# Input slices of 2, 2, 4, 4 and 4 blocks, more partial sums, wide products and new distances in a hybrid RWKV-7 and attention block

## The chip, the cores and the metric

The kernel runs on one core of a Trainium2 chip. The metric is the time of one execution in microseconds (us) on the device; the times shown are medians of several executions. The core's engines are named as the profile names them: PE multiplies matrices (PEld is its loading of weights), DVE is the vector engine, ACT the scalar engine, POOL the general one, SP issues most of the DMA transfers.

## What is computed

One sequence of 256 tokens with 2048 channels passes through one block, in float32:

```python
mod = silu(c) @ w_ada + b_ada                 # (2048) x (2048, 12288)
sh1, sc1, gt1, sh2, sc2, gt2 = split(mod, 6)
h = rms_norm(x) * (1 + sc1) + sh1
p = h @ w_in + b_in                           # (256, 2048) x (2048, 8736)
y_rwkv = rwkv7_branch(p[:, :3360], ...)       # 16 heads of 64: r, k, v; low ranks for decay, rate, gate
y_attn = sliding_window_attention(p[:, 3360:4640])   # 16 query heads, 2 key/value heads, window 128
g_rwkv, g_attn = split(sigmoid(p[:, 4640:]), 2)
merged = g_rwkv * (y_rwkv @ w_branch_rwkv) + g_attn * (y_attn @ w_branch_attn)
x = x + gt1 * (merged @ w_out)
h = rms_norm(x) * (1 + sc2) + sh2
x = x + gt2 * (square(relu(h @ w_up)) @ w_down)      # 2048 -> 8192 -> 2048
out = rms_norm(x)
```

The RWKV recurrence over 256 steps is done in chunks of 64 tokens; within a chunk a triangular system is inverted, first in blocks of 16.

## The kernel before

**Products.** Every weight matrix is read once, in tiles of 0.52 MB (four blocks of 128 rows by 256 columns, or two by 512). `split` (L269) loads such a tile (raw, L290), ACT rounds it into whi (L278), and DVE subtracts to get the remainder wlo (L279); there are seven buffers for raw, which the tiles of w_ada share, and four each for whi and wlo. The activations are kept as two parts too (hA and hB, side by side in one tile h). `feed` (L282) then issues for each 128x128 piece three matmuls of 256 columns (L301): whi by the high part, whi by the low part, wlo by the high part. This is the narrow form, 24 matmuls a tile, and gates, keys and branches use it through `cols_product`. The up projection of the MLP uses a wide form (`up_pair`, L1173): whi by both parts at once, 512 columns, and wlo by the high part, 16 matmuls a tile; the two halves of the result are added afterwards, by a copy on ACT (L1191) and an add on DVE (L1192) for each 128 columns.

**Input slices.** h depends on sc1 and sh1, which come from w_ada. So the 16 blocks of 128 channels are taken in slices, `SL`. For the first slice PE multiplies the ada tiles (L204); for the later ones DVE accumulates them (`ada_dve`, L223) while PE works on the slice before, and PE adds up the columns at the end (L190). Each slice contributes to 16 column pairs of w_in (256 columns each). Six are kept in PSUM throughout (three tiles each with two pairs), and ten are summed in SBUF (`sums`): a product over the slice's blocks only, copied by ACT in the first slice (L974) and added by DVE later (L976).

**Streams beside the products.** The modulation of the next slice, the attention and the RWKV branch are generators. `pulse` is called once a tile and advances each by a rate (`RATE_ADA`, `RATE_ATT`, `RATE_RW`, `RATE_BG`), so their instructions stand among those of the products; on each engine the order is then fixed. After the fourth sum of the last slice the heads of the RWKV branch and the attention begin.

**After the slices** come gates 4 to 6, `keyed(2)` and `keyed(3)` (k, r and v of the later head groups, written to a DRAM buffer that the second half of the RWKV branch reads), gate 7, eight pairs of an attention gate and an attention branch product, eight RWKV branch products, w_out, and the MLP.

**The inverse.** `inverse16` (L615) runs twice, once in each half of the RWKV branch. The blocks of 16 are written to a DRAM buffer scr, read back as lg, worked on by 31 small operations on POOL (L626, L628, L630; 15 to 64 elements per partition, then 256), written to DRAM and read back as in; then PE uses them (L651).

Of the kernel before, what the change touches and what calls it, by code (L numbers as in the profile page):

```python
# [85 lines left out]
def hybrid_block(ctx: ExitStack, tc, x, c, w_ada, b_ada, norm1_gain, w_in, b_in, rwkv_mix, rwkv_w0,  # L86
# [181 lines left out]

    def split(nk, width, load):  # L269

        step = max(1, 1024 // width)
# [10 lines left out]
    def feed(w, k0, nk, cols, blocks, xh, xl, begin, end, tw=T):  # L282
# [11 lines left out]
        for a, n, hi, lo in split(nk, width, load):  # L294
            for wt, xs in ((hi, (xh, xl)), (lo, (xh,))):
                for kk in range(n):
                    k = k0 + a + kk
                    o = 0
                    for ps, j, m in blocks:
                        for xx in xs:  # L300
                            TE.matmul(ps[0:m, j * tw:(j + 1) * tw], lhsT=wt[:, kk, o:o + m], rhs=xx(k),  # L301
                                      start=(k == begin and xx is xh and wt is hi and j == 0),
                                      stop=(k == end and wt is lo), skip_group_check=True)
                        o += m
# [303 lines left out]
    def zero_inverses():  # L608
        z = arena[0][:, 2 * W3:2 * W3 + BP // 2]
        G.memset(z, 0.0)  # L610
        for n in range(2):
# [678 lines left out]
```

## Time and profile before

| | us |
|---|---|
| median of 3 executions | 1543.69 |
| lowest and highest | 1542.36, 1549.06 |
| the profiled execution's own time | 1539.98 |
| its span in the trace | 1538.2 |
| PE busy | 1477.7 |
| DVE busy | 1119.0 |
| ACT busy | 724.0 |
| POOL busy | 40.1 |

The span is what the trace covers of the execution; a busy time is the union of an engine's instructions, and what is missing to the span is idle. The mean granted clock of PE was 0.988. The windows further below cut the span at the first w_in product (40.68 us), at the starts of the next slices (91.46, 143.13, 193.5), and behind the RWKV branch products (711); from 711 on come w_out and the MLP.

### The profile page before, as it was taken

Reading aid. Unit: us, or ns where it says so; the run is one execution under the profiler, and the core shown is the slowest. Engines: PE = TensorE matmul, PEld = TensorE weight load, DVE = VectorE, ACT = ScalarE, POOL = GpSimd, SP = SyncE. Lnnn points to the kernel's source line nnn. Section 1 sums busy time; section 2 is a strip of 40 time slices with the busy share of each in tenths; the row PEclk is TensorE's granted clock in tenths of the full one; section 3 lists DMA queues with packets and bytes.
Section 4 is the critical chain, followed back from the end, with each engine's and each line's share of the span. In section 5 each row is a group of like instructions: output and inputs, shape, how many; then the busy total and the mean of one; then the engine's idle time right before and its main releaser. Section 6 shows DMA issues by size and latency. Waiting matters only on the chain.

```text
span 1538.2 us, 28406 instructions
## 1 busy us (share of the span) xinstructions
PE 1477.7 (96%) x11194; PEld 1313.8 (85%) x11194; DVE 1119.0 (73%) x1842; ACT 724.0 (47%) x1136; POOL 40.1 (3%) x97
## 2 busy tenths in 40 slices
PE   5899999999999989999899999999999999999997
PEld 2898998998998989899789888888888888888885
DVE  1989979977688948768679765766676675655676
ACT  3354477656364424444457544434344343444443
POOL 2000000030000030000000000000000000000000
PEclk9899999999999999999999999999999999999999
DMA  9999977779898768879775777677776776666652
GB/s 345 338 342 306 350 237 229 239 200 316 251 291 282 239 182 296 269 255 310 246 236 165 241 230 236 213 233 231 228 231 213 236 231 204 190 191 193 203 183 79
DMA packets 297093, 372.68 MB, mean 242 GB/s; under 512 B 40912, under 2 KB 198384, under 8 KB 296320
## 3 DMA queue, kind: packets, MB, share of 16 engines
q1 hardware_dynamic: 296448, 370.72, 75.8%
q8 instruction: 88, 1.44, 0.4%
q0 software_dynamic: 512, 0.15, 0.1%
q14 instruction: 45, 0.37, 0.1%
HBM read 357.96 MB, written 12.86 MB: 241 GB/s over the span
## 4 chain that ended last, share of the span: by engine, by line
PE 84%; DVE 6%; DMA 4%; issue 2%; ACT 2%; POOL 1%; SPq 0%; DVEq 0%; POOLq 0%; ACTq 0%
PE mm L1173 21%; PE mm L301 19%; PE mm L323 14%; PE ax L323 14%; PE ax L301 7%; DMA ada<-in_w_ada_dram 2%; DVE acc L223 2%; DVE wlo L279 1%; PE ax L690 1%; PE ax L484 1%; PE ax L190 1%; PE ax L573 1%; DMA raw<-in_w_in_dram 1%; DMA tt<-in_x_dram 0%; POOL p L628 0%
## 5 line engine op out<-in xcount | busy, mean ns | idle before, releaser
L278 ACT CAST whi<-raw 128x1024 fp32r<-128x1024 f32 x458 | 478.9, 1049 | 591.1 <-PE ax L323 220.2
L279 DVE TENSOR_TENSOR wlo<-raw,whi 128x1024 fp32r<-128x1024 f32 x458 | 556.6, 1219 | 210.3 <-ACT whi L278 206.2
L223 DVE SCALAR_TENSOR_TENSOR acc<-ada,cact,acc 128x512 f32<-128x512 f32 x330 | 247.1, 749 | 90.7 <-DMA ada<-in_w_ada_dram 86.3
L1173 PE MATMUL mm<-h,whi 128*128 128x512 f32 x928 | 235.0, 395 | 0.0
L301 PE MATMUL mm<-h,whi 128*128 128x256 f32 (+1 forms) x1440 | 196.9, 285 | 3.4 <-ACT whi L278 3.4
L1173 PEld LDWEIGHTS mm<-h,whi 128*128 128x128 f32 x928 | 166.2, 188 | 31.5
L301 PEld LDWEIGHTS mm<-h,whi 128*128 128x128 f32 (+1 forms) x1440 | 178.0, 189 | 9.7 <-issue 3.5
L323 PE MATMUL mm<-whi,u 128*128 128x512 f32 x512 | 137.3, 390 | 0.0
L323 PE MATMUL ax<-whi,u 128*128 128x512 f32 x512 | 136.9, 389 | 0.0
L1173 PEld LDWEIGHTS mm<-h,wlo 128*128 128x128 f32 x928 | 123.2, 188 | 10.5
L1173 PE MATMUL mm<-h,wlo 128*128 128x256 f32 x928 | 124.8, 277 | 0.0
L301 PE MATMUL ax<-h,whi 128*128 128x256 f32 x768 | 105.7, 286 | 8.8 <-DVE p L976 5.1
L323 PEld LDWEIGHTS ax<-whi,u 128*128 128x128 f32 x512 | 96.1, 188 | 20.0
L323 PEld LDWEIGHTS mm<-whi,u 128*128 128x128 f32 x512 | 95.4, 188 | 19.4
L301 PEld LDWEIGHTS ax<-h,whi 128*128 128x128 f32 x768 | 96.9, 192 | 11.1 <-ACT whi L278 6.6
L301 PE MATMUL mm<-h,wlo 128*128 128x256 f32 (+1 forms) x720 | 103.7, 281 | 0.0
L301 PEld LDWEIGHTS mm<-h,wlo 128*128 128x128 f32 (+1 forms) x720 | 92.4, 189 | 0.4 <-DVE wlo L279 0.2
L323 PE MATMUL ax<-wlo,u 128*128 128x512 f32 x256 | 78.8, 389 | 0.0
L323 PE MATMUL mm<-wlo,u 128*128 128x512 f32 x256 | 78.8, 389 | 0.0
L301 PE MATMUL ax<-h,wlo 128*128 128x256 f32 x384 | 57.9, 283 | 0.1
L323 PEld LDWEIGHTS ax<-wlo,u 128*128 128x128 f32 x256 | 48.0, 188 | 10.0
L323 PEld LDWEIGHTS mm<-wlo,u 128*128 128x128 f32 x256 | 48.1, 188 | 10.0
(350 smaller groups left out, 1668.0 us busy)
## 6 DMA issues: line engine op xcount, KB each, us to landing
ada<-in_w_ada_dram SPq DMA_DIRECT2D x192, 512.0 KB, 5.6
raw<-in_w_up_dram SPq DMA_DIRECT2D x128, 512.0 KB, 4.1
raw<-in_w_down_dram SPq DMA_DIRECT2D x128, 512.0 KB, 4.2
raw<-in_w_in_dram SPq DMA_DIRECT2D x72, 512.0 KB, 5.7
raw<-in_w_in_dram SPq DMA_DIRECT2D x128, 256.0 KB, 5.7
raw<-in_w_out_dram SPq DMA_DIRECT2D x32, 512.0 KB, 5.0
raw<-in_w_branch_attn_dram SPq DMA_DIRECT2D x16, 512.0 KB, 6.0
raw<-in_w_branch_rwkv_dram SPq DMA_DIRECT2D x16, 512.0 KB, 5.3
```

The source lines that it names most:

```text
L190: TE.matmul(ps[:, j:j + 1], lhsT=acc[:, j * P:(j + 1) * P], rhs=ones[:, 0:1], start=True, stop=True)
L223: V.scalar_tensor_tensor(o, in0=t[:, a, :], scalar=ck, in1=o, op0=ALU.mult, op1=ALU.add)
L278: S.copy(hi[:], raw[:])
L279: V.tensor_tensor(lo[:], raw[:], hi[:].bitcast(F32), op=ALU.subtract)
L301: TE.matmul(ps[0:m, j * tw:(j + 1) * tw], lhsT=wt[:, kk, o:o + m], rhs=xx(k), start=(k == begin and xx is xh and wt is hi and j == 0), sto ...
L323: TE.matmul(pss[tb][:], lhsT=uu(k)[:, sl], rhs=wt[:, kk, :], start=(first and k == 0), stop=(final and k == kblocks - 1))
L484: TE.matmul(out[hs, :], lhsT=src[hs, chunk(c)], rhs=ident[hs, hs], start=True, stop=True)
L573: TE.matmul(pT[hs, o:o + P], lhsT=src[hs, chunk(c)], rhs=ar[hs, i, c].rearrange("p a b -> p (a b)"), start=True, stop=True)
L690: TE.matmul(ps[hs, j, i, part, :], lhsT=lhs(j, i, hs), rhs=rhs(j, i, hs), start=(first and j == 0 and i == 0), stop=True, skip_group_check ...
L1173: TE.matmul(pss[j][:, 0:w_], lhsT=wt[:, kk, j * P:(j + 1) * P], rhs=xx(a + kk), start=(a + kk == 0 and wt is hi), stop=(a + kk == KC - 1 a ...
```

## The change

The input is taken in five slices, the first two of two blocks. Ada tiles of a slice of two hold four blocks of rows by 256 columns instead of two by 512. Three pairs join the sums, those of `keyed(2)`; after the last slice they go to the DRAM buffer, and the later product goes. For slices of four, `feed` takes one pair at a time, and with `apart=True` it finishes one PSUM bank before it starts the next. The heads start after the third sum of the last slice, the attention after the seventh. `both_product` is the wide form for any matrix; the gates, both branches and the up projection use it, while `keyed(3)` and the 32 columns of `gd2` stay narrow. Three of the attention gates are made earlier and kept in DRAM. The 31 small operations of the inverse move from POOL to DVE. A gap of 16 floats stands between whi and wlo, and one tile (`ss2`) is allocated later, so some distances between buffers change by 64 bytes. Some rates change.

```diff
-SL = (4, 4, 4, 4)
-RATE_ADA = 1.5
-RATE_RW = 1.7
+NLATE = 2
+SL = (2, 2, 4, 4, 4)
+RATE_ADA = 1.0
+RATE_RW = 2.05
-RATE_BG = (0.9, 0.3, 0.4, 0.2)
+RATE_BG = (1.05, 0.3, 0.4, 0.2)
-PAD_H, PAD_A, PAD_Z = 112, 16, 96
+PAD_W, PAD_H, PAD_A, PAD_Z = 16, 112, 16, 96
...
             hi = wp.tile([P, m, width], F32R, tag="whi", bufs=4, name=nm("whi"))
+            if not padded:
+                padded.append(wp.tile([P, PAD_W], F32, tag="pad_w", bufs=1, name="pad_w"))
             lo = wp.tile([P, m, width], F32R, tag="wlo", bufs=4, name=nm("wlo"))
...
+        groups = [[b for b in at if b[1] is ps] for _, ps, j, _ in at if j == 0] if apart else [at]
...
         for a, n, hi, lo in split(nk, width, load):
-            for wt, xs in ((hi, (xh, xl)), (lo, (xh,))):
...
+            for group in groups:
+                for wt, xs in ((hi, (xh, xl)), (lo, (xh,))):
+                    for kk in range(n):
+                        k = k0 + a + kk
+                        for o, ps, j, m in group:
+                            for xx in xs:
...
+    def both_product(w, kblocks, c0, xh, xhl, t):
+        pss = [ps_mm(), ps_mm()]
...
+        for a, n, hi, lo in split(kblocks, 2 * P, load):
+            for wt, xx, w_ in ((hi, xhl, 2 * T), (lo, xh, T)):
+                for kk in range(n):
+                    for j in range(2):
+                        TE.matmul(pss[j][:, 0:w_], lhsT=wt[:, kk, j * P:(j + 1) * P], rhs=xx(a + kk),
+                                  start=(a + kk == 0 and wt is hi), stop=(a + kk == kblocks - 1 and wt is lo),
+                                  skip_group_check=True)
+            pulse(0.5)
+        for j, ps in enumerate(pss):
+            tj = t[:, j * T:(j + 1) * T]
+            S.copy(tj, ps[:, 0:T])
+            V.tensor_tensor(tj, ps[:, T:], tj, op=ALU.add)
...
+    keys = [((n, ss), o + 256 * ss) for ss in (2,) for n, o in (("k", O_K), ("r", O_R), ("v", O_V))]
...
         yield
+        yield
         for s in range(15):
...
-            G.tensor_tensor(t_, a16[:, s, m:16].unsqueeze(2).broadcast_to([P, n, m]),
+            V.tensor_tensor(t_, a16[:, s, m:16].unsqueeze(2).broadcast_to([P, n, m]),
                             x16[:, 0, s:s + 1, 0:m].broadcast_to([P, n, m]), op=ALU.mult)
-            G.tensor_tensor(x16[:, 0, m:16, 0:m], x16[:, 0, m:16, 0:m], t_, op=ALU.add)
+            V.tensor_tensor(x16[:, 0, m:16, 0:m], x16[:, 0, m:16, 0:m], t_, op=ALU.add)
...
-        G.tensor_copy(x16[:, 1], x16[:, 0].rearrange("p a b -> p b a"))
+        V.tensor_copy(x16[:, 1], x16[:, 0].rearrange("p a b -> p b a"))
...
-        for _ in range(5):
+        for _ in range(4):
             yield
...
-                while len(spilled - {'gd2'}) < 7:
+                while not {(ss_, n) for ss_ in (2, 3) for n in range(3)} <= spilled:
                     yield
...
         if qT is None:
+            while ("q", q2) not in spilled:
+                yield
...
-        for g2 in range(0, len(sums), 2):
...
+        for g0 in range(0, len(sums), 4 // nk):
+            some = sums[g0:g0 + 4 // nk]
+            ps = [ps_ax() for _ in some]
+            feed(w_in, k0, nk, [(c, 256) for _, c in some], [(p, j, P) for p in ps for j in range(2)],
+                 hA, hB, k0, k0 + nk - 1, apart=True)
...
-            if last and g2 == 2:
-                finish(bg)
-                begin_heads()
-                begin_attention()
-                rate["rw"], rate["att"] = RATE_RW, RATE_ATT
+                    elif n > 1:
+                        keys_out(n, "krv".index(what), o)
+                    spilled.add((what, n))
+                    if (what, n) == ("v", 1):
+                        finish(bg)
+                        begin_heads()
+                        rate["rw"] = RATE_RW
+                    if (what, n) == ("q", 1):
+                        begin_attention()
+                        rate["att"] = RATE_ATT
...
     def gates(g):
-        ps = cols_product(w_in, KC, O_GR + g * 256, [P, P], hA, hB)
-        gate_out(g, tl("gr", (2, T), 3), ps)
+        t = tl("gr", (2, T), 3)
+        both_product(w_in, KC, (O_GR if g < 8 else O_GA - 2048) + g * 256, hA, hAB, flat(t))
+        gate_out(g, t, flat(t))
...
-    for g in left[:3]:
+    for g in range(NSUM, 8):
         gates(g)
-    for ss in range(2, 4):
-        keyed(ss)
-        if ss == 3:
-            finish(att)
-            gd2()
-            spilled.add("gd2")
-    for g in left[3:8 - NSUM]:
-        gates(g)
...
+    keyed(3)
+    for g in range(NLATE):
+        gates(8 + g)
+    finish(att)
+    gd2()
+    spilled.add("gd2")
+    gates(8 + NLATE)
...
-        gate_of(8 + g, t, cols_product(w_in, KC, O_GA + g * 256, [P, P], hA, hB))
+        if g <= NLATE:
+            nc.sync.dma_start(flat(t), grd[8 + g])
+        else:
+            both_product(w_in, KC, O_GA + g * 256, hA, hAB, flat(t))
+            gate_of(8 + g, t, flat(t))
...
-        ps = cols_product(w_branch_attn, 8, g * 256, [P, P], yh, yl)
-        V.scalar_tensor_tensor(flat(t), in0=flat(t), scalar=1.0, in1=ps[:], op0=ALU.add, op1=ALU.mult)
+        s = tl("gr", (2, T), 3)
+        both_product(w_branch_attn, 8, g * 256, yh, yhl, flat(s))
+        V.scalar_tensor_tensor(flat(t), in0=flat(t), scalar=1.0, in1=flat(s), op0=ALU.add, op1=ALU.mult)
...
-        ps = cols_product(w_branch_rwkv, 8, g * 256, [P, P], yh, yl)
+        s = tl("gr", (2, T), 3)
+        both_product(w_branch_rwkv, 8, g * 256, yh, yhl, flat(s))
...
-    ss2 = ml.tile([P, 16], F32, name="ss2")
...
+    ss2 = ml.tile([P, 16], F32, name="ss2")
...
-                for j, ps in enumerate(up_pair(g * 1024 + c2 * 256)):
-                    tj = t[:, j * T:(j + 1) * T]
-                    S.copy(tj, ps[:, 0:T])
-                    V.tensor_tensor(tj, ps[:, T:], tj, op=ALU.add)
+                both_product(w_up, KC, g * 1024 + c2 * 256, hA, hAB, t)
```

The first place is the start of the program in SP's queue. `ada` is a tile of w_ada, `raw` a tile of w_in. Before, from the third last of the 16 ada tiles that stand ahead of the first raw one:

```order
L145 DMA ada_299<-in_w_ada_dram 128x2x512
L145 DMA ada_303<-in_w_ada_dram 128x2x512
L145 DMA ada_307<-in_w_ada_dram 128x2x512
L290 DMA raw_339<-in_w_in_dram 128x2x256 x2
L145 DMA ada_371<-in_w_ada_dram 128x2x512
L290 DMA raw_375<-in_w_in_dram 128x2x256 x2
L145 DMA ada_406<-in_w_ada_dram 128x2x512
```

After, from the fourth of the ada tiles:

```order
L146 DMA ada_107<-in_w_ada_dram 128x4x256
L146 DMA ada_263<-in_w_ada_dram 128x4x256
L146 DMA ada_269<-in_w_ada_dram 128x4x256
L146 DMA ada_281<-in_w_ada_dram 128x4x256
L146 DMA ada_287<-in_w_ada_dram 128x4x256
L300 DMA raw_313<-in_w_in_dram 128x2x256 x2
L146 DMA ada_346<-in_w_ada_dram 128x4x256
L300 DMA raw_352<-in_w_in_dram 128x2x256 x2
```

The first raw tile moved up by eight ada tiles; behind it one ada tile stands between two raw ones as before.

The second place is the first of the two inverses. Before, POOL does nothing else there (`rs` is a scratch tile, `p` the inverse):

```order
L626 TENSOR_TENSOR rs_3852<-lg_3849,p_522_3851 128x15
L628 TENSOR_TENSOR p_522_3851<-p_522_3851,rs_3852 128x15
L626 TENSOR_TENSOR rs_3852<-lg_3849,p_522_3851 128x28
L628 TENSOR_TENSOR p_522_3851<-p_522_3851,rs_3852 128x14x2
L626 TENSOR_TENSOR rs_3852<-lg_3849,p_522_3851 128x39
L628 TENSOR_TENSOR p_522_3851<-p_522_3851,rs_3852 128x13x3
```

After, on DVE, where the L661 and L663 are the same operations, L284 makes wlo, L224 is an ada step, L875 and L876 belong to the attention's softmax and L341 is the add of a wide product:

```order
L284 TENSOR_TENSOR wlo_4314<-raw_4311,whi_4313 128x1024
L224 SCALAR_TENSOR_TENSOR acc_4093<-ada_4379,cact,acc_4093 128x512 x2
L661 TENSOR_TENSOR rs_4129<-lg_4126,p_585_4128 128x15
L284 TENSOR_TENSOR wlo_4360<-raw_4357,whi_4359 128x1024
...
L663 TENSOR_TENSOR p_585_4128<-p_585_4128,rs_4129 128x15
L284 TENSOR_TENSOR wlo_4404<-raw_4401,whi_4403 128x1024
L875 TENSOR_SCALAR m_4167<-m_4167 128x4
L876 TENSOR_TENSOR m_4167<-sinkb,m_4167 128x4
L661 TENSOR_TENSOR rs_4129<-lg_4126,p_585_4128 128x28
L341 TENSOR_TENSOR gr_4062<-mm_4063,gr_4062 128x256
L663 TENSOR_TENSOR p_585_4128<-p_585_4128,rs_4129 128x14x2
```

The inverse now stands in line with splits, ada steps, attention and adds. In SP's queue, at the same place, `lg` is what the first L661 reads, and L614 writes the last part of `scr`:

```order
L981 DMA grd<-gr_3726 128x512
L655 DMA p_585_4128<-consts_dram 128x256
L146 DMA ada_4333<-in_w_ada_dram 128x2x512
L328 DMA raw_4357<-in_w_in_dram 128x4x256
L614 DMA scr<-tt_3477 64x4x64 x2
L146 DMA ada_4379<-in_w_ada_dram 128x2x512
L328 DMA raw_4401<-in_w_in_dram 128x4x256
L652 DMA lg_4126<-scr 128x16x16
```

The read of lg stands behind the load of raw_4401, and DVE's first operation on it ahead of the split of raw_4357.

The third place is PE in a product of h with w_in. Before, in the fourth gate of that stage (`mm` is a PSUM bank that holds both halves):

```order
L301 MATMUL mm_5195<-h_219,whi_5198 128x256 x16
L301 MATMUL mm_5195<-h_219,wlo_5199 128x256 x8
L301 MATMUL mm_5195<-h_220,whi_5232 128x256 x16
L301 MATMUL mm_5195<-h_220,wlo_5233 128x256 x8
L301 MATMUL mm_5195<-h_221,whi_5266 128x256 x16
L301 MATMUL mm_5195<-h_221,wlo_5267 128x256 x8
```

After, in an attention gate, with one bank for each half of the columns:

```order
L334 MATMUL mm_5415<-h_215,whi_5419 128x512
L334 MATMUL mm_5416<-h_215,whi_5419 128x512
L334 MATMUL mm_5415<-h_215,whi_5419 128x512
L334 MATMUL mm_5416<-h_215,whi_5419 128x512
...
L334 MATMUL mm_5415<-h_215,wlo_5420 128x256
L334 MATMUL mm_5416<-h_215,wlo_5420 128x256
L334 MATMUL mm_5415<-h_215,wlo_5420 128x256
L334 MATMUL mm_5416<-h_215,wlo_5420 128x256
```

Eight matmuls of 512 columns and eight of 256 stand where 24 of 256 stood.

## Rows read from the trace of the kernel before

**Rows 1.** The page's head: the span, then each engine's busy time and instructions.

```profile
span 1538.2 us, 28406 instructions
...
PE 1477.7 (96%) x11194; PEld 1313.8 (85%) x11194; DVE 1119.0 (73%) x1842; ACT 724.0 (47%) x1136; POOL 40.1 (3%) x97
```

**Rows 2.** Windows: length; busy PE, PEld, DVE, ACT, POOL; PEclk; DMA share; GB/s.

```profile
0.00:40.68 40.68, 22.05 (x116) 8.81 (x116) 8.87 (x36) 16.00 (x23) 9.63 (x23) 0.94 0.98 346
40.68:91.46 50.78, 46.44 (x358) 45.59 (x358) 43.63 (x58) 23.21 (x32) 0.00 (x0) 0.91 1.00 338
91.46:143.13 51.67, 48.42 (x405) 47.48 (x404) 46.96 (x64) 22.17 (x28) 0.00 (x0) 1.00 0.98 326
143.13:193.50 50.37, 47.45 (x403) 46.72 (x402) 48.05 (x65) 19.81 (x24) 0.00 (x0) 1.00 1.01 334
193.50:711.00 517.50, 501.50 (x5709) 472.58 (x5708) 408.84 (x904) 267.57 (x547) 30.51 (x74) 0.99 0.82 255
```

**Rows 3.** Timeline 0 to 45 us: start, duration, engine, line, operation, [idle before].

```profile
16.90 3.95 PE L408 MATMUL ax<-kt,tt 128*128 128x128 f32 x32 [1.30 <-ACT tt L401]
...
37.36 0.16 DVE L192 TENSOR_TENSOR sh<-ax,colC 128x4 f32<-128x4 f32 x1 [9.41 <-PE ax L190]
```

**Rows 4.** Timeline of PE alone at 668, 685 and 1040 us: whi matmuls of tiles.

```profile
668.11 1.98 PE L301 MATMUL mm<-tt,whi 128*128 128x256 f32 x16
...
670.83 1.98 PE L301 MATMUL mm<-tt,whi 128*128 128x256 f32 x16
...
685.53 2.05 PE L301 MATMUL mm<-tt,whi 128*128 128x256 f32 x16
...
688.36 1.81 PE L301 MATMUL mm<-tt,whi 128*128 128x256 f32 x14
...
1040.49 2.02 PE L1173 MATMUL mm<-h,whi 128*128 128x512 f32 x8
...
1043.27 2.02 PE L1173 MATMUL mm<-h,whi 128*128 128x512 f32 x8
```

**Rows 5.** Timeline of DVE at 171 us; groups by form: count | busy, mean ns.

```profile
171.16 1.28 DVE L976 TENSOR_TENSOR p<-ax,p 128x512 f32<-128x512 f32 x2
172.36 1.22 DVE L279 TENSOR_TENSOR wlo<-raw,whi 128x1024 fp32r<-128x1024 f32 x1
173.50 1.53 DVE L223 SCALAR_TENSOR_TENSOR acc<-ada,cact,acc 128x512 f32<-128x512 f32 x2
174.94 1.22 DVE L279 TENSOR_TENSOR wlo<-raw,whi 128x1024 fp32r<-128x1024 f32 x1
...
L445 DVE SCALAR_TENSOR_TENSOR in<-p,colA,in 128x255 f32<-128x255 f32 x6 | 2.7, 479 | 0.1
...
L1192 DVE TENSOR_TENSOR tt<-mm,tt 128x256 f32<-128x256 f32 x58 | 21.7, 416 | 0.0
...
L1191 ACT COPY tt<-mm 128x256 f32<-128x256 f32 x58 | 18.5, 370 | 0.0
```

**Rows 6.** Timeline 544 to 573 us: the inverse on POOL, and PE behind it.

```profile
544.85 0.71 POOL L626 TENSOR_TENSOR rs<-lg,p 128x15 f32<-128x15 f32 x1 [42.59 <-DMA lg<-scr]
...
560.07 0.61 POOL L630 COPY p<-p 128x256 f32<-128x256 f32 x1
...
567.22 0.30 PE L651 MATMUL ax<-in,tt 64*64 64x64 f32 x2 [2.42 <-DMA in<-scr]
...
568.51 1.95 PE L651 MATMUL ax<-in,tt 64*64 64x64 f32 x32 [0.99 <-DMA in<-scr]
...
571.34 1.97 PE L651 MATMUL ax<-in,tt 64*64 64x64 f32 x30 [0.88 <-DMA in<-scr]
```

**Rows 7.** DMA issues by kind: count, KB each, median us to landing.

```profile
scr<-tt SPq DMA_DIRECT2D x16, 64.0 KB, 2.3
...
lg<-scr SPq DMA_DIRECT2D x2, 128.0 KB, 4.3
```

**Rows 8.** The page's costliest groups: busy us, mean ns | idle before, what ended it.

```profile
L279 DVE TENSOR_TENSOR wlo<-raw,whi 128x1024 fp32r<-128x1024 f32 x458 | 556.6, 1219 | 210.3 <-ACT whi L278 206.2
```

More of the change, by code (lines that the diff above doesn't have):

```diff
@@ L280, in split, with feed @@
             yield a, m, hi, lo
[L282 removed]
+    def feed(w, k0, nk, cols, blocks, xh, xl, begin, end, tw=T, apart=False):
         width = sum(m for _, _, m in blocks)
+        at, o = [], 0
+        for ps, j, m in blocks:
+            at.append((o, ps, j, m))
+            o += m
+        groups = [[b for b in at if b[1] is ps] for _, ps, j, _ in at if j == 0] if apart else [at]
         def load(raw, a, m):
@@ L294, in feed @@
         for a, n, hi, lo in split(nk, width, load):
-            for wt, xs in ((hi, (xh, xl)), (lo, (xh,))):
[L296 to L304, printed above, removed]
+            for group in groups:
[4 more added lines that the diff above has]
+                            for xx in xs:
+                                TE.matmul(ps[0:m, j * tw:(j + 1) * tw], lhsT=wt[:, kk, o:o + m], rhs=xx(k),
+                                          start=(k == begin and xx is xh and wt is hi and j == 0),
+                                          stop=(k == end and wt is lo), skip_group_check=True)
             pulse(0.5)
@@ L438, in hybrid_block @@
     rest = [(t_s1, 0), (t_s1, 1), (t_s2, 0), (t_s2, 1)] + rest
+    arena = [tl("a1", (8 * T,)), tl("a2", (8 * T,))]
+    rest[3:3] = [(arena[0].rearrange("p (a b) -> p a b", b=T), i) for i in range(len(keys) + 1)]
+    del rest[3 + len(keys) + 1]
     def shifted(dst, ps, m, j):
@@ L797, in rwkv @@
             last = [norm(ss + j, sts[j]) for j in range(2)]
-        yr["hi"] = tl("tt", (8, T), 2, F32R)
-        yr["lo"] = tl("tt", (8, T), 2, F32R)
+        yr["t"] = [tl("tt", (4, 2, T), 2, F32R) for _ in range(2)]
         y0 = tl("ar", (4, T), 2)
@@ L918, in begin_attention @@
             att.append(pair(q2, q0 if q2 == 0 else None))
-    for _ in range(8):
+    for _ in range(4):
         next(first)
@@ L964, in hybrid_block @@
                  hA, hB, 0, KC - 1)
-        for g2 in range(0, len(sums), 2):
-            two = sums[g2:g2 + 2]
-            ps = [ps_ax() for _ in two]
-            feed(w_in, k0, nk, [(c, 256) for _, c in two], [(p, j, P) for p in ps for j in range(2)],
-                 hA, hB, k0, k0 + nk - 1)
-            for a, ((what, n), _) in enumerate(two):
-                t, j = rest[g2 + a]
+        for g0 in range(0, len(sums), 4 // nk):
[3 more added lines that the diff above has]
+                 hA, hB, k0, k0 + nk - 1, apart=True)
+            for a, ((what, n), _) in enumerate(some):
+                t, j = rest[g0 + a]
                 o = flat(t, j)
```

45 lines of the change are left out of this document (18 added, 27 removed).

## The prediction

> **What bounds the kernel now.** I read the page's head first. TensorE (PE) is busy in 1477.7 of 1538.2 us [rows 1], so only 60.5 us can be had by filling gaps; beyond that, PE's own work would have to become shorter. Then the busy time by stage [rows 2] says where the 60.5 us lie: 18.6 before the first product of w_in (40.68 − 22.05), 4.3, 3.3 and 2.9 in the first three input slices, 16.0 from 193.5 to 711 (last slice, gates, keys, both branches), and what is left, 15.4, in the rest, where little is changed. The reader is to see in the same rows that the limits differ by stage. In the start DMA moves 346 GB/s at a share of 0.98 while PE is half idle. In a slice three engines end together: DMA share 0.98 to 1.01, PE busy 46.4 to 48.4, VectorE (DVE) 43.6 to 48.1 of about 51 us. In the middle PE is busy 97%, DVE 79%, DMA 82%: PE is the bound and the others have slack.
>
> **1. The start.** Sixteen ada tiles of 0.52 MB are landed before the first product; in the queue's order after the change there are eight. At the 346 GB/s of this stretch [rows 2], 8 × 0.524 = 4.2 MB are 12.1 us. What is on PE stays: the transposes of x start at 16.90 and take 4 us, then come the ada products, and the last sum for sh is taken at 37.36 [rows 3], 3.3 us before the first product. With half the columns these steps shrink little. I take −10.5 (first product at 30.2); bounds −12.1, and −8 if PE's work behind the transposes' end at 20.9 holds it.
>
> **2. The slices.** Per block nothing is free: moving from 10 to 13 pairs makes 19 instead of 16 tiles in a slice of four, 9.5 in a slice of two. I work each limit out.
> - PE: a tile takes 2.83 us from start to start (685.53 to 688.36 [rows 4]). Sixteen are 45.3, and the windows show 47.9 (mean of the last two, [rows 2]), so 2.6 go to the column sums of ada. Nineteen: 53.8 + 2.6 = 56.4; a slice of two: 26.9 + 1.8 = 28.7.
> - DVE: from start to start a split is 1.14 (172.36 to 173.50), an ada step of 512 is 0.72 (173.50 to 174.94, two steps), an add into a sum is 0.60 (171.16 to 172.36, two adds) [rows 5]. Check on the slice of before: 16 × 1.14 + 32 × 0.72 + 10 × 0.60 = 47.3, where 47.0 and 48.1 were seen. After, in a slice of four: 19 × 1.14 + 23.0 + 13 × 0.60 = 52.5. First slice of two (32 ada steps of 256 columns; between half of 0.72 and the 0.479 that an operation on 255 columns takes [rows 5]; no adds): 24 to 27. Second slice of two, which must make the modulation of a slice of four: 11.4 + 23.0 + 7.8 = 42.2.
> - DMA at 334 GB/s: 9.2, 13.4, 18.4, 18.4 MB are 27.5, 40, 55, 55 us.
>
> So the two slices of four are bound by PE as closely as by DMA; their old gap was 2.9 to 3.3, and with 1.4 and 3.9 of slack on the two others I take 57.5. The second slice of two is short of PE work by 13 us; its buffers allow no lead of that size. I take 42. For the first I take 31, since PE's clock was 0.91 there [rows 2] and 28.7/0.91 is 31.5. End: 30.2 + 31 + 42 + 115 = 218.2 instead of 193.5, +24.7. The last slice has 3 tiles more, 3 × 2.83 = +8.5. Later keyed(2) is gone, 12 × 2.80 = −33.6 (2.80 lies between the two narrow paces of [rows 4], 2.72 and 2.83). **Net −0.4.** The lower bound is a start and slices without any gap, by PE alone 30.2 + 28.7 + 28.7 + 112.8 = 200.4, by DMA alone (59.3 MB at 346 GB/s) 201.6: 17 better, **−17.6**. The upper bound is slices of four with 6% of PE idle, as in the windows of before: 60 each, **+5**.
>
> **3. Wide products.** Of the eighty tiles each carries the same columns (16 × 256 + 8 × 256 before, 8 × 512 + 8 × 256 after). A wide tile takes 2.78 from start to start (1040.49 to 1043.27), a narrow one 2.72 or 2.83 [rows 4]: 80 × (+0.06 … −0.05) = −4 … +4.8, I take 0. [...]
>
> What is added is 2 copies and 2 adds of 256 columns for each of 28 products: 56 × 0.370 = 20.7 us on ScalarE (ACT, 268 of 517 busy: hidden) and 56 × 0.416 = 23.3 us on DVE [rows 5]. DVE's sum for the middle: 408.8 + 3 × 1.22 + 3 × 0.69 − 12 × 1.22 (keyed(2)) + 23.3 + 12.4 (inverses, below) = 436, with PE's 501.5 + 8.5 − 33.6 = 476.4. The DVE-to-PE ratio rises from 0.82 to 0.91; in the slices, where it is 0.97 to 1.01, PE idled 5.8 to 6.4% ([rows 2]: 3.25 of 51.67, 2.92 of 50.37), in the middle 3.1%. I take a value halfway, 4.7%: 476.4/0.953 = 499.9, of which 23.5 are idle instead of 16.0: **+7.5**. Bounds: 3.1% gives 491.6, −0.8; 6.0% gives 506.8, idle 30.4, +14.4. What hides the adds today is DVE's 108 us of slack there; after, 64 are left.
>
> **4. The inverse.** On POOL a chain of 31 operations runs from 544.85 to 560.68, 15.8 us, and PE's first matmul of the levels starts at 567.22 after gaps of 2.42, 0.99 and 0.88 [rows 6]: 4.3 us in all, the only PE wait that this chain ends. No row shows these operations on DVE. Bounds: 0.16 (128x4, [rows 3]) and 0.479 (128x255); the sizes are 15 to 64, so 0.2, which for 62 gives 12.4 us of DVE. Removed at best: −4.3. Against it stands the order shown with the change: on DVE the first operation of the inverse has to wait for the write of scr and the read of lg, 2.3 + 4.3 us [rows 7], and splits, ada steps and the attention's operations stand behind it. On POOL that wait held nothing. In SP's queue the read stands behind the load of raw_4401, while DVE wants it ahead of the split of raw_4357, one tile earlier. If the loads run two or more tiles ahead of the splits, the read has landed when DVE gets there, and it costs 0; if not, up to 6.6 per inverse, 13 for two. I take 0 (−4.3 … +13), since the seven buffers of raw and ada let the loads run ahead.
>
> **5. New distances.** Only addresses move by 64 bytes. What the trace shows of such effects is that the same narrow code runs at 2.72 and at 2.83 [rows 4]; over 80 tiles that is ±9 us either way. I take 0.
>
> **Sum.** −0.4 + 7.5 = +7. The profiled execution took 1539.98 (span 1538.2), 3.7 below the median 1543.69; I add the 7 to the median: **1551**.
>
> **The rivals.**
> - B, slower: DVE in program order becomes the middle's bound. An operation of the inverse waits for its DRAM read, the splits queue behind it, PE runs out of wlo. In favour: DVE at 87% of the middle, PE's 6% idle where DVE was fuller still, and the read's place in SP's queue. Against: of the 210.3 us that DVE idles before splits, 206.2 end with ACT's whi and next to none with a load [rows 8], so raw tiles are there ahead of time. Price 14.4 + 13 − 0.4 = +27: 1571. It decides once the read of lg lands later than the first inverse operation's turn. [...]
> - C, faster: the slices run without gaps (−17.6), DVE's extra work stays hidden (−0.8) and the inverse's stall goes (−4.3): −22.7, 1521. In favour: 346 GB/s is sustained in the start; PE's share is 97% with DVE at 79%. Against: in three slices nobody reached less than 2.9 of idle, and the second short slice lacks PE work.
> - D: the pace of the streams changes through forms or distances, by 0.1 us a tile: ±9, 1543 to 1560 around the sum.
> - That the change doesn't do what it says I exclude: the queue's order shows eight ada rows and DVE's the inverse.
>
> **Chances.** A (the sum) 0.42, its own range 1541 to 1561: slower 0.19, same 0.21, faster 0.02. B 0.18, all slower. C 0.30, all faster. D 0.10: faster 0.04, same 0.04, slower 0.02. About half a per cent, 7.7 us, is what a measurement of this kernel can tell from no change. So faster 0.36, same 0.25, slower 0.39. The range runs from 1521, C's middle (half of C below it would be 0.15, but C reaches up to A's edge, so I count 0.1), to 1569 just below B's sum (0.1 above it).
>
> **What would show it.** First w_in product near 30; slice starts near 61, 103, 161, 218; PE idle in the second slice of two of about 13 us (none: C). PE idle of the middle, 3.1% (C), 4.7% (A) or 6% (B). Before the inverse's first operation on DVE an idle time ended by the DMA of lg, with PE waiting for wlo right after it (B), or none. DVE's durations for 15 to 64 columns near 0.2. Narrow tiles at 2.72 or 2.83 against wide at 2.78. The prediction is wrong if slices of two cost PE no gap, or if the pace of the streams changes over more than the eighty tiles.

## The result and the profile after

The changed kernel takes 1565.13 us (median), the kernel before 1543.03 us in the same comparison: a ratio of 1.0135, 95% interval 1.0104 to 1.0166. It is slower by about 21 us. The profiled execution's span is 1565.3 us. The page's head of the changed kernel, as in [rows 1]:

```profile
span 1565.3 us, 27267 instructions
...
PE 1501.1 (96%) x10554; PEld 1302.4 (83%) x10554; DVE 1167.7 (75%) x2016; ACT 742.6 (47%) x1198; POOL 12.2 (1%) x35
```

The number of weight tiles is the same but for one, and yet PE is busy 23.4 us longer, most of the 27.1 by which the spans differ; its idle time rose only from 60.5 to 64.2. DVE's 48.7 us more come from the adds of the wide form, the inverse, the adds of the sums, and the ada steps of the second slice, which DVE now makes. The windows of the changed kernel by stage answer to [rows 2]; the first row names the columns (x instructions). The slices begin at 31.33, 63.34, 108.40, 168.68 and 225.76, w_out at 737.07, what follows it at 834.11:

```profile
core 0: us, PE busy (x) PEld busy (x) DVE busy (x) ACT busy (x) POOL busy (x), PEclk, DMA share, GB/s
0.00:31.33 31.33, 14.99 (x108) 9.46 (x108) 7.21 (x33) 14.98 (x21) 9.33 (x23) 1.00 0.95 302
31.33:63.34 32.01, 30.55 (x236) 29.98 (x237) 27.60 (x49) 16.91 (x25) 0.00 (x0) 0.95 0.98 318
63.34:108.40 45.06, 36.77 (x247) 33.28 (x246) 40.91 (x59) 14.45 (x20) 0.00 (x0) 0.91 0.94 304
108.40:168.68 60.28, 58.90 (x473) 58.50 (x473) 56.49 (x77) 25.54 (x32) 0.00 (x0) 0.95 0.97 317
168.68:225.76 57.08, 56.39 (x475) 56.28 (x474) 52.52 (x71) 23.05 (x28) 0.00 (x0) 1.00 0.98 320
225.76:737.07 511.31, 485.91 (x4812) 420.47 (x4811) 421.00 (x1011) 273.38 (x592) 2.91 (x12) 0.97 0.80 250
737.07:834.11 97.04, 97.04 (x459) 79.82 (x457) 73.20 (x104) 48.50 (x76) 0.00 (x0) 1.00 0.75 256
834.11:1565.30 731.19, 720.53 (x3757) 614.62 (x3755) 488.77 (x618) 325.82 (x411) 0.00 (x0) 1.00 0.65 206
```

Two windows of the kernel before for the last two, which [rows 2] does not hold:

```profile
711.00:814.07 103.07, 98.45 (x459) 81.21 (x457) 73.51 (x103) 48.59 (x74) 0.00 (x0) 0.98 0.72 241
814.07:1538.20 724.13, 713.35 (x3757) 611.38 (x3755) 489.18 (x618) 326.65 (x411) 0.00 (x0) 1.00 0.67 208
```

Stage by stage, in us, from the two profiled executions (their spans differ by 27.1, the medians by 22.1):

| | before | change | difference |
|---|---|---|---|
| to the first product | 40.7 | 31.3 | −9.4 |
| slices but the last | 152.8 | 194.4 | +41.6 |
| last slice to w_out | 517.5 | 511.3 | −6.2 |
| w_out | 103.1 | 97.0 | −6.0 |
| after w_out | 724.1 | 731.2 | +7.1 |
| sum | 1538.2 | 1565.3 | +27.1 |

The reader should stop at the last stage. Its tiles and its order are those of before, its granted clock is 1.00 as before, and still PE is busy 7.2 us longer. The timeline of PE in the changed kernel shows why, as [rows 4] did for before: two narrow tiles of a slice, two wide ones of the up projection, two of the down projection, each row the first whi matmuls of a tile.

```profile
174.40 2.08 PE L311 MATMUL mm<-h,whi 128*128 128x256 f32 x16
...
177.26 2.08 PE L311 MATMUL mm<-h,whi 128*128 128x256 f32 x16
...
1009.66 2.00 PE L334 MATMUL mm<-h,whi 128*128 128x512 f32 x8
...
1012.44 2.00 PE L334 MATMUL mm<-h,whi 128*128 128x512 f32 x8
...
1015.22 1.09 PE L353 MATMUL mm<-whi,u 128*128 128x512 f32 x4
...
1018.00 1.09 PE L353 MATMUL mm<-whi,u 128*128 128x512 f32 x4
```

A narrow tile comes every 2.86 us (before 2.72 or 2.83), a wide one every 2.78, a down tile every 2.77 to 2.78, where the trace of before has 2.72:

```profile
1015.95 1.07 PE L323 MATMUL mm<-whi,u 128*128 128x512 f32 x4
...
1018.67 1.07 PE L323 MATMUL mm<-whi,u 128*128 128x512 f32 x4
```

The first inverse on DVE, timeline, with the splits (L284) that stand between its operations:

```profile
352.71 0.17 DVE L661 TENSOR_TENSOR rs<-lg,p 128x15 f32<-128x15 f32 x1
352.86 1.22 DVE L284 TENSOR_TENSOR wlo<-raw,whi 128x1024 fp32r<-128x1024 f32 x1
...
357.99 0.18 DVE L663 TENSOR_TENSOR p<-p,rs 128x15 f32<-128x15 f32 x1
358.08 1.22 DVE L284 TENSOR_TENSOR wlo<-raw,whi 128x1024 fp32r<-128x1024 f32 x1
...
359.35 0.18 DVE L661 TENSOR_TENSOR rs<-lg,p 128x28 f32<-128x28 f32 x1
```

The operations take 0.17 to 0.18 us there, and no idle time stands ahead of the first: lg had landed. What PE waited for between the last slice and w_out (us in total, times, longest):

```profile
PE ax L686 <- DMA in<-scr: 7.6, 4, 3.3
...
PE mm L334 <- DVE wlo L284: 2.3, 4, 1.5
```

PE waits 7.6 for the inverse's reads, where it waited 4.3 before [rows 6], and only 2.3 for wlo.

### The profile page after: what moved, and what is told of

Its sections match the earlier page's. It is cut to its first block, busy times and chain, and to the rows that moved or that the text cites. A ratio compares the mean times of both kernels' runs of the same rounds, so it can differ in the third digit from the quotient of the medians.

```text
span 1565.3 us, 27267 instructions
## 1 busy us (share of the span) xinstructions
PE 1501.1 (96%) x10554; PEld 1302.4 (83%) x10554; DVE 1167.7 (75%) x2016; ACT 742.6 (47%) x1198; POOL 12.2 (1%) x35
## 4 chain that ended last, share of the span: by engine, by line
PE 85%; DVE 8%; DMA 3%; issue 2%; ACT 2%; SPq 0%; DVEq 0%; ACTq 0%
PE mm L334 31%; PE mm L353 14%; PE ax L353 14%; PE ax L311 10%; PE mm L311 5%; DVE wlo L284 2%; DVE acc L224 2%; PE ax L725 2%; PE ax L191 1%; PE ax L518 1%; PE ax L607 1%; DMA scr<-p 1%; PE ax L695 1%; ACT whi L283 1%; DMA tt<-in_x_dram 1%
## 5 line engine op out<-in xcount | busy, mean ns | idle before, releaser
L284 DVE TENSOR_TENSOR wlo<-raw,whi 128x1024 fp32r<-128x1024 f32 x459 | 556.4, 1215 | 203.0 <-ACT whi L283 199.5
L334 PE MATMUL mm<-h,whi 128*128 128x512 f32 x1312 | 337.6, 396 | 0.0
L224 DVE SCALAR_TENSOR_TENSOR acc<-ada,cact,acc 128x512 f32<-128x512 f32 (+1 forms) x360 | 261.1, 725 | 50.9 <-DMA ada<-in_w_ada_dram 46.7
L334 PEld LDWEIGHTS mm<-h,whi 128*128 128x128 f32 x1312 | 234.1, 188 | 44.5 <-issue 2.2
L334 PEld LDWEIGHTS mm<-h,wlo 128*128 128x128 f32 x1312 | 177.2, 189 | 15.7 <-DVE wlo L284 3.4
L334 PE MATMUL mm<-h,wlo 128*128 128x256 f32 x1312 | 182.0, 281 | 2.0 <-DVE wlo L284 2.0
L311 PE MATMUL ax<-h,whi 128*128 128x256 f32 x960 | 136.6, 289 | 5.5 <-DVE a L1012 1.2
L353 PEld LDWEIGHTS mm<-whi,u 128*128 128x128 f32 x512 | 95.5, 188 | 22.1
L311 PE MATMUL mm<-h,whi 128*128 128x256 f32 (+1 forms) x480 | 70.8, 290 | 3.1 <-ACT whi L283 2.4
L311 PEld LDWEIGHTS ax<-h,wlo 128*128 128x128 f32 x480 | 64.5, 193 | 4.7 <-DVE wlo L284 4.7
L311 PEld LDWEIGHTS mm<-h,whi 128*128 128x128 f32 (+1 forms) x480 | 63.3, 191 | 4.4 <-ACT whi L283 2.5
L311 PE MATMUL mm<-h,wlo 128*128 128x256 f32 (+1 forms) x240 | 39.0, 290 | 0.2 <-DVE wlo L284 0.2
```

Of the source, the lines that this page charges most:

```text
L224: V.scalar_tensor_tensor(o, in0=t[:, a, :], scalar=ck, in1=o, op0=ALU.mult, op1=ALU.add)
L284: V.tensor_tensor(lo[:], raw[:], hi[:].bitcast(F32), op=ALU.subtract)
L334: TE.matmul(pss[j][:, 0:w_], lhsT=wt[:, kk, j * P:(j + 1) * P], rhs=xx(a + kk), start=(a + kk == 0 and wt is hi), stop=(a + kk == kblocks ...
L353: TE.matmul(pss[tb][:], lhsT=uu(k)[:, sl], rhs=wt[:, kk, :], start=(first and k == 0), stop=(final and k == kblocks - 1))
```

## The experiments

Each is the change or the kernel before with a small edit. Ratios are to the kernel before, timed beside it on the same chip. L numbers in rows are those of each run's own file.

**1. Both distances undone in the change.**

```diff
-            if not padded:
-                padded.append(wp.tile([P, PAD_W], F32, tag="pad_w", bufs=1, name="pad_w"))
...
+    ss2 = ml.tile([P, 16], F32, name="ss2")
     x1 = ml.tile([P, 2, D], F32, name="x1")
...
     V.tensor_scalar(gtc[:, 0:KC], gtc[:, 0:KC], 0.5, None, op0=ALU.mult)
-    ss2 = ml.tile([P, 16], F32, name="ss2")
```

> The change without the gap of 16 floats between whi and wlo and with ss2 back at its old place; all else as in the change. If the distances slow the streams of PE, the tile of the down projection goes back from 2.77 to 2.72 us from start to start (128 tiles, about 6.5 us) and the narrow tile of the slices from 2.86 towards 2.83 (about 2 us): some 1557, ratio to before about 1.009. If the distances do nothing, both paces stay and the time is that of the change, about 1565, ratio 1.0135.

Measured: 1549.02 us, ratio 1.0046 (1.0023 to 1.0069). PE and DVE run the same instructions in the same order, only addresses differ. Its windows, by the same stages (the two short slices in one):

```profile
0.00:31.30 31.30, 15.34 (x109) 9.81 (x109) 7.29 (x33) 15.01 (x21) 9.36 (x23) 1.00 0.93 302
31.30:105.70 74.40, 64.17 (x481) 59.59 (x482) 68.51 (x107) 30.60 (x43) 0.00 (x0) 0.97 0.97 315
105.70:164.20 58.50, 57.12 (x474) 56.72 (x474) 56.19 (x77) 25.65 (x33) 0.00 (x0) 0.95 1.00 332
164.20:219.70 55.50, 54.81 (x475) 54.70 (x474) 52.58 (x71) 23.80 (x28) 0.00 (x0) 1.00 1.01 333
219.70:724.80 505.10, 484.56 (x4813) 418.99 (x4812) 421.38 (x1011) 273.35 (x592) 2.92 (x12) 0.97 0.81 253
724.80:821.20 96.40, 96.40 (x459) 79.79 (x458) 72.78 (x104) 48.46 (x76) 0.00 (x0) 1.00 0.75 256
821.20:1545.20 724.00, 713.32 (x3757) 611.35 (x3755) 488.39 (x618) 326.56 (x411) 0.00 (x0) 1.00 0.65 208
```

And two down tiles of it:

```profile
1014.89 1.07 PE L351 MATMUL mm<-whi,u 128*128 128x512 f32 x4
...
1017.61 1.07 PE L351 MATMUL mm<-whi,u 128*128 128x512 f32 x4
```

2.72 is back. Against the change the slices are 6.1 shorter, the middle 6.2, w_out 0.6, the rest 7.2: 20.1 us between the two traces, 14 (0.89%) between the timed ratios. PE's busy time is 15.4 less (1501.1 against 1485.7), close to the timed 14; 6.5 of it lie in the slices and 7.2 behind w_out. Of the middle's 6.2 only 1.4 are busy time, the rest is idle time. The distances cost more than expected, and they are two thirds of the loss by the timed runs.

**2. Four slices of four in the change.**

```diff
-SL = (2, 2, 4, 4, 4)
-RATE_ADA = 1.0
+SL = (4, 4, 4, 4)
+RATE_ADA = 1.5
...
-    for _ in range(4):
+    for _ in range(8):
         next(first)
```

> The change with four slices of four again, the old rate for ada (1.5) and the old number of early steps; thirteen sums, wide products, inverse on DVE and distances as in the change. If the two slices of two are what costs, the start loses 9 to 10 us, but the gap of 8 us in the second short slice goes and four slices of about 58 us follow 40.7: last slice begins near 214 instead of 226, about 1553, ratio 1.006. If what costs is thirteen sums rather than the slices' form, the last slice begins within 3 us of 226 and the time stays at 1565.

Measured: 1557.2 us, ratio 1.0104 (1.0075 to 1.0132). The last slice begins at 218.5 instead of 225.8, where 214 was expected; the ratio expected was 1.006. The interval overlaps that of the change, so by itself this run does not settle the slices' form; run 8 adds to it.

**3. The inverse back on POOL in the change.**

```diff
-            V.tensor_tensor(x16[:, 0, m:16, 0:m], x16[:, 0, m:16, 0:m], t_, op=ALU.add)
+            G.tensor_tensor(x16[:, 0, m:16, 0:m], x16[:, 0, m:16, 0:m], t_, op=ALU.add)
```

and the same for the multiplication ahead of it and the last copy; one pause less ahead of the loop and one more behind it, as before.

> The change with the inverse's 31 operations on POOL, with its pauses as before; all else as in the change. If DVE's program order is what costs (rival B of the prediction), the middle from the last slice to w_out loses 7 to 13 us and the ratio to before falls to about 1.006. If the inverse is not the cause, the POOL chain of 16 us comes back and the time stays within 4 us of the change, or is slower by that: ratio 1.011 to 1.017.

Measured: 1578.18 us, ratio 1.0242 (1.0212 to 1.0272), 1.07% slower than the change. Both theories had the size wrong, and rival B also the sign. PE's longest waits in the middle of this run:

```profile
PE ax L685 <- DMA in<-scr: 13.0, 2, 12.0
PE ax L893 <- ACT a L888: 10.4, 1, 10.4
```

One read of the inverse is waited for 12.0 us at a stretch. The window around it (columns as above) shows PE busy half of the time, at a granted clock of 0.72, while POOL is busy 9.2:

```profile
590.00:620.00 30.00, 15.47 (x221) 14.09 (x221) 10.36 (x16) 4.70 (x7) 9.23 (x21) 0.72 0.70 165
```

That is the second inverse. The wait of 10.4 belongs to the first, by way of the DMA queue. SP issues the write of the inverse (scr<-p), and what stands behind it in the queue, only when POOL is done:

```profile
SPq L663 <- POOL p L662: 29.8, 2, 15.8
...
350.09 0.46 SPq L300 DMA_DIRECT2D raw<-in_w_in_dram  x1
364.60 0.37 SPq L663 DMA_DIRECT2D scr<-p  x1
...
366.03 1.15 SPq L146 DMA_DIRECT2D ada<-in_w_ada_dram  x1
...
371.03 1.54 DVE L224 SCALAR_TENSOR_TENSOR acc<-ada,cact,acc 128x512 f32<-128x512 f32 x2 [9.95 <-DMA ada<-in_w_ada_dram]
...
373.55 0.48 PE L893 MATMUL ax<-kt,a 128*128 128x128 f32 x1 [10.44 <-ACT a L888]
```

Between 350.09 and 364.60, for 14.5 us, SP issues nothing. The ada tile behind the write comes late, DVE stands idle before the step that reads it, the softmax operations of the attention stand behind that step, and PE waits for them. In the change SP waits 8.1 us in all at this write. So in the changed order the move to DVE is a gain of some 16 us, not a cost.

**4. Narrow products in the change's gates and branches.**

```diff
-        both_product(w_in, KC, (O_GR if g < 8 else O_GA - 2048) + g * 256, hA, hAB, flat(t))
-        gate_out(g, t, flat(t))
+        gate_out(g, t, cols_product(w_in, KC, (O_GR if g < 8 else O_GA - 2048) + g * 256, [P, P], hA, hB))
```

and the same for the other gates and the branches.

> The change with the gates and both branches as narrow products again (24 matmuls of 256 a tile, the result read from PSUM, no copies and adds); the up projection stays wide. If the adds on DVE cost (DVE 421 us busy in the middle, 23 of them adds), DVE falls to about 398 and the time by about 7 us, ratio 1.009. If the form is free, the time follows the two paces alone, 80 tiles between 2.72 and 2.86 against 2.78: from 5 us less to 6 more, ratio 1.010 to 1.017.

Measured: 1561.48 us, ratio 1.0126 (1.0090 to 1.0162). The form makes no difference that this can tell.

**5. Only the gap undone in the change.**

```diff
-            if not padded:
-                padded.append(wp.tile([P, PAD_W], F32, tag="pad_w", bufs=1, name="pad_w"))
```

> The change without the gap of 16 floats between whi and wlo, with ss2 still at its new, later place. If the gap alone slows the streams, the down tile is at 2.72 again and the time that of the run without both (ratio 1.005). If the place of ss2 does it for the stages that follow it (w_out, MLP), the slices and the middle go back to 2.83 and 2.72 but the down tile stays at 2.77: some 7 us more, ratio 1.009.

Measured: 1551.76 us, ratio 1.0047 (1.0024 to 1.0069). The narrow tiles are at 2.72 and 2.83 again, as without both; the down tiles are at 2.75, between 2.72 and 2.78. The gap is most of the cost; the place of ss2 has a part in the MLP, 128 × 0.03 = 4 us in the trace, too little for the timed runs to show.

**6. Nothing but the two distances in the kernel before** (the edit of run 1 the other way round).

> The kernel before with nothing but the two new distances. If distances act by themselves, the narrow tiles of the slices and the middle (some 115 tiles, at 2.72 or 2.83 before) come to 2.86 and the down tiles to 2.77: 0.03 to 0.14 a tile, about 8 us, and 128 x 0.05 = 6.5 us, together 12 to 15: ratio 1.008 to 1.010. If they matter only together with the other parts of the change, the time stays within 4 us of before, ratio 0.998 to 1.002.

Measured: 1555.08 us, ratio 1.0071 (1.0048 to 1.0094). Its down tiles:

```profile
1016.77 1.09 PE L327 MATMUL mm<-whi,u 128*128 128x512 f32 x4
...
1019.54 1.09 PE L327 MATMUL mm<-whi,u 128*128 128x512 f32 x4
```

2.77, and its narrow tiles are at 2.86. The distances cost 11 us by themselves.

**7. Nothing but the inverse on DVE in the kernel before** (the edit of run 3 the other way round).

> The kernel before with nothing but the inverse moved to DVE. The run of the change with the inverse back on POOL was slower by about 1.1%. If the move helps by itself, the stage from 193.5 to 711 shortens by 4 to 10 us (the gaps at the inverse's reads, 4.3 us, and the tail of 16 us on POOL): ratio 0.993 to 0.997. If the inverse on DVE only helps where few products are left to cover the chain, as in the change, the time stays within 4 us: 0.998 to 1.002.

Measured: 1539.52 us, ratio 0.9973 (0.9941 to 1.0005). Not settled: its profiled execution was 4 us longer than that of before, its median is 5 shorter than the median beside it. A gain of 16 is excluded.

**8. The change with neither the distances nor the slices of two** (the edits of runs 1 and 2).

> The change without both distances and with four slices of four: thirteen sums, wide products, inverse on DVE and the later order of gates remain. If slices of two and distances cost independently of each other (about 0.3% and 0.9% so far), the ratio is 1.000 to 1.003. If with the faster streams the slices of two are no longer limited by anything but the first loads, they gain and this run is slower than the one without distances: above 1.005.

Measured: 1541.52 us, ratio 0.9970 (0.9947 to 0.9993). Faster than both kernels. Beside run 1, the slices of two (with the rate and the early steps of run 2) cost 0.8%, 12 us, with the two intervals some 5 us either way; the change beside run 2 gives 0.3%, 5 us, with intervals that overlap. The traces give less: 5.8 at the start of the last slice (219.7 against 213.9), 3.5 at the end. Two windows late in its middle:

```profile
590.00:620.00 30.00, 25.09 (x431) 22.57 (x431) 16.51 (x25) 8.04 (x17) 0.00 (x0) 0.79 0.85 239
...
650.00:680.00 30.00, 25.39 (x153) 17.89 (x152) 20.36 (x84) 14.54 (x32) 0.00 (x0) 0.82 0.58 189
```

PE idles 4.9 and 4.6 us there and gets a clock of 0.79 and 0.82: the inverse and the chains of the second half, and the last norms, with few product tiles beside them.

**9. Run 8 with narrow gates and branches** (the edits of runs 4 and 8).

> The change with four slices of four, without both distances, and with gates and branches narrow again. Beside the same kernel with wide products (ratio 0.997) this tells what the wide form is worth where the narrow pace is 2.72 or 2.83 and not 2.86. If the form is free, the difference is 80 tiles x (-0.05 to +0.06), at most 5 us: 0.994 to 1.000. If the adds and copies on DVE and ACT lengthened the middle, it is below 0.993; if wide is the better form, above 1.001.

Measured: 1541.34 us, ratio 0.9990 (0.9971 to 1.0009). The form is free again, to 0.2 or 0.3%, with the intervals overlapping.

**10. Run 8 with a faster RWKV stream.**

```diff
-RATE_RW = 2.05
+RATE_RW = 2.5
```

> The change with four slices of four, without both distances, and RATE_RW at 2.5 instead of 2.05, so that the RWKV branch ends earlier. If its exposed end costs (idle of 4.9 and 4.6 us in 590 to 620 and 650 to 680, at granted clocks of 0.79 and 0.82), the stretch from the last slice to w_out falls from 505 to 495 and the ratio to 0.991. If its length is set by its own chain of dependences, the same idle appears elsewhere and the ratio stays at 0.995 to 0.999.

Measured: 1536.92 us, ratio 0.9976 (0.9961 to 0.9992), the same as run 8. The norms no longer stand idle, but the exposed part moved forward:

```profile
550.00:590.00 40.00, 34.33 (x178) 28.84 (x176) 35.69 (x76) 13.59 (x21) 0.00 (x0) 0.91 0.96 286
590.00:620.00 30.00, 27.40 (x629) 24.57 (x630) 16.48 (x33) 8.91 (x18) 0.00 (x0) 0.89 0.79 250
```

PE idles 5.7 and 2.6 us in these two, 2.1 and 4.9 in run 8. In the trace the stretch from the last slice to w_out is 499.0 long (213.44 to 712.48), 6 shorter than in run 8, where 10 were expected, but the timed runs do not tell the two kernels apart. The ratio of 0.991, expected if the rate shortens the exposed end, is excluded; whether the chain's own length sets all of what is left stays open.

**11. Run 8 with ten sums.**

```diff
-    keys = [((n, ss), o + 256 * ss) for ss in (2,) for n, o in (("k", O_K), ("r", O_R), ("v", O_V))]
+    keys = [((n, ss), o + 256 * ss) for ss in () for n, o in (("k", O_K), ("r", O_R), ("v", O_V))]
...
-    keyed(3)
+    for ss in (2, 3):
+        keyed(ss)
```

> The change with four slices of four, without both distances, and with ten sums instead of thirteen (keyed(2) as a product behind the gates again). If the three sums cost where the slices are limited by three engines at once, the last slice begins near 194 instead of 214 and the middle grows by 34 - 8 = 25 less than that gap: 2 to 6 us faster, ratio 0.993 to 0.996. If the sums are free, 0.996 to 0.999. If they helped (keys earlier, so that the second half of the RWKV branch starts earlier), above 1.000.

Measured: 1560.46 us, ratio 1.0124 (1.0104 to 1.0144). The last slice begins at 196.7, 17.2 earlier than in run 8, though nine tiles of 2.8 us, 25 in all, were taken out ahead of it; the window from there to w_out is 543.3, 38 longer:

```profile
196.70:740.00 543.30, 513.33 (x5045) 447.60 (x5044) 445.23 (x1039) 283.34 (x601) 2.86 (x12) 0.96 0.81 256
```

25 of the 38 are the product that came back (12 − 3 tiles of 2.8). PE idles 30.0 there, against 18.5 in run 8 (505.3 − 486.8), and 10.9 in the slices ahead of the last, against 5.6. So the three sums fill PE's gaps in the slices and spare idle time later: they are worth 1.5%, 24 us, in this order of work. Part of that may be that with ten sums the attention starts only one sum after the heads; that was not tried apart. Ten sums, four slices and the distances are those of the kernel before, and yet run 11 is 1.24% slower than that, some 19 us. The rest of the change costs them where the three sums are missing: the order of the gates, the starts of the streams, the rates, wide products, the inverse on DVE. The wide form is free by runs 4 and 9, and the inverse on DVE is no cost by runs 3 and 7; the others were not tried apart.

**12. Run 10 with a gap of 32 floats.**

```diff
-PAD_W, PAD_H, PAD_A, PAD_Z = 16, 112, 16, 96
+PAD_W, PAD_H, PAD_A, PAD_Z = 32, 112, 16, 96
```

> The kernel of the run with RATE_RW 2.5 (four slices of four, ss2 at its old place), with a gap of 32 floats, 128 bytes, between whi and wlo where that run has none and the change has 16 floats. The order on every engine is that of the run with RATE_RW 2.5. If any gap slows the streams, the down tile is at 2.77 and the narrow tile at 2.86, and the ratio at 1.004 to 1.008. If it is the 64 bytes that do it and 128 don't, the paces stay at 2.72 and 2.83 or below and the ratio at 0.996 to 0.999.

Measured: 1540.64 us, ratio 0.9991 (0.9973 to 1.0009). Two narrow tiles of a slice and two down tiles:

```profile
177.58 1.98 PE L311 MATMUL ax<-h,whi 128*128 128x256 f32 x16
...
180.30 1.86 PE L311 MATMUL ax<-h,whi 128*128 128x256 f32 x15
...
1015.65 1.09 PE L353 MATMUL mm<-whi,u 128*128 128x512 f32 x4
...
1018.43 1.09 PE L353 MATMUL mm<-whi,u 128*128 128x512 f32 x4
```

Neither expectation holds: most narrow tiles are at 2.72 (none at 2.83), the wide ones at 2.75, and the down tiles at 2.78. So none of the gaps tried is the best for all three forms.

## Why the prediction was right or wrong

The forecast was 1551, slower, range 1521 to 1569. The time is 1565: the direction and the range hold, the loss is three times the forecast one, and the step that failed is number 5.

**Distances (step 5): wrong, the step that decides.** It took 0, with ±9, and counted eighty tiles. The runs show 14 us in the change (run 1) and 11 in the kernel before (run 6), since the gap lies between the buffers that every product reads: 128 down tiles alone are some 7. The mechanism was named (rival D, and the prediction's last sentence on the pace of the streams, by which it is wrong); the term was mis-sized, because [rows 4] held two paces of one form and none of the down projection, and because only the eighty tiles that change their form were counted. That 1565 lies in the range is luck: D's own range ended at 1560, and the range's upper end came from B, which had the sign wrong.

Nor are the 2.72 and 2.83 of [rows 4] an effect of addresses alone, as step 5 read them. In the kernel before, the tiles of the RWKV branch products come every 2.72 up to 676.27 and every 2.83 from 682.71 on, with the same four pairs of buffers. Between the two paces stand the eight matmuls of one column that add up ada columns:

```profile
678.99 0.95 PE L190 MATMUL ax<-kt,acc 128*128 128x1 f32 x8
```

Of the sixteen tiles of these products, the five ahead of the eight matmuls take 2.72 each, the one right behind them 2.91, and the ten after that 2.82 or 2.83. Why the pace changed there was not shown.

**The sum without it: right in total, by terms that cancel.** Run 1 is the change without step 5, and it measures +0.46%, 7 us: the sum's +7. That the terms cancel so well is luck. By its windows:
- Start: −9.4, forecast −10.5.
- Slices: the last begins at 219.7, forecast 218.2. The second short slice of the change leaves PE 8.3 idle (45.06 − 36.77), forecast 13.
- Middle: 505.1, forecast 499.9. The idle share is 4.1% (20.5 of 505.1; 5.0% in the change), forecast 4.7%; PE's work is 484.6, forecast 476.4. The prediction has no term for the clock of the middle: the granted clock was 0.97 there, before 0.99 [rows 2], and as an estimate two hundredths of 485 us are some 10, enough for the 8.2 that are missing.
- w_out: −6.7, forecast nothing. Before, PE had one idle time of 4.6 in it, ahead of the transposes of x, a granted clock of 0.98 and, in its first part, tiles of 2.80; all three are gone in run 1. Run 9, with narrow branch products ahead of w_out, has tiles of 2.80 again, run 8, with wide ones, has none. Where the idle time went was not tried.

**Slices of two: not forecast apart.** They don't pay: the start's 9 us are lost again in the slices, and 0.8% in all by runs 1 and 8 (0.3%, not clear of noise, by the change and run 2). The sum took slices and sums together (net −0.4); apart, the sums gain (run 11) and the short slices lose.

**Wide products: their 0 is right, the +7.5 for a fuller DVE is not shown.** Runs 4 and 9 find no difference that can be told. DVE's middle is 421 busy, forecast 436; without the adds it is 406 in run 4 and 405 in run 9, and PE's idle time there has no common direction: 16.9 where the change has 25.4, 20.5 where run 8 has 18.5.

**Inverse: rival B had the sign wrong, and −4.3 was no bound in the new order.** DVE's operations take 0.2 as taken, nothing waits for lg, PE waits 2.3 for wlo. PE's wait for the inverse's reads did not go, it rose from 4.3 to 7.6, so the sum's 0 was some 3 short. In the changed order the move all the same saves 16 us (run 3). The bound came from the wait that the POOL chain caused in the kernel before. There PE's products ran for 20 us beside the second chain (544.85 to 564.8); in run 3 they run for 12 (583.8 to 596.3), and the same chain of 16 us is waited for 12.0. At the first inverse the chain costs PE 10.4 through SP's queue, a path that the prediction did not look at. SP waited for POOL in the kernel before too, but PE had no single wait over 3.7 from 193.5 to 711:

```profile
SPq L629 <- POOL p L628: 24.8, 2, 14.1
```

A cover was read from the old order and not counted again for the new one. Twice an operation on DVE starts only behind what stands ahead of it. In the change the inverse's second operation starts at 357.99, 5.3 us after the first, behind the split and the attention's operations that stand ahead of it. In run 3 a softmax operation (L882) whose input ACT had done at 361.83 starts at 372.48, behind the ada step that waits.

**Rival C: partly there.** Without short slices and distances the change is faster, by 0.3% (run 8), not by 1.5%. The slices were not free of gaps: PE idles 12.3 in those ahead of the last in run 1 and 5.6 in run 8.

## What to carry to other kernels

Price a few bytes between two buffers over every tile that reads them, in each form of product, and read the pace from tile to tile in all stages. Here the two distances of 64 bytes made 1 to 5% of a narrow tile's time (2.83 to 2.86, 2.72 to 2.86) and 2% of a down tile's (2.72 to 2.77). When products are moved, count anew what is left beside each serial chain, since the chain's old wait is no bound for its new one, and look in the DMA queue for what waits behind the chain's result. Take a change of many parts apart: here two parts that gain about 16 and 24 us in this order, though not against the kernel before, stood beside one that loses about 14 and one that loses 5 to 12.

## What the runs showed of the hardware

The time from tile to tile, at a granted clock of 1.00, with the same matmuls and nothing waited for (most tiles of each run):

| gap between whi and wlo, place of ss2 | narrow | wide | down |
|---|---|---|---|
| none, old (before, runs 1, 7 to 11) | 2.72 and 2.83 | 2.77 | 2.72 |
| none, later (run 5) | 2.72 and 2.83 | 2.77 | 2.75 |
| 64 bytes, later (the change, runs 2 to 4, 6) | 2.86 | 2.78 | 2.77 |
| 128 bytes, old (run 12) | 2.72 | 2.75 | 2.78 |

What in the distance decides, and why one narrow code has two paces at one distance, stays open: no run varied one address alone over a range, and none varied what stands between two stretches of tiles.

In windows where PE was left with the short matmuls of a chain and gaps, the granted clock was lower than in those on either side: 0.72 in 590 to 620 of run 3, between two of 1.00; 0.79 in 590 to 620 of run 8, between 1.00 and 0.98. Idle time alone did not lower it: in the first 31.33 us of the change PE is busy 14.99, at 1.00. As an estimate, if busy time goes with the clock, some 4 of the 15.47 us that PE is busy in the window of run 3 (0.28 × 15.47) came on top of its waits.
